# Paired PSUM banks, a sum of squares on VectorE and Newton steps for 1/sqrt in a hybrid decoder layer

## The chip, the core and the metric

The kernel runs on one core of one Trainium2 chip. The metric is device time in microseconds. PE is TensorE (matrix products), PEld its loading of weights, DVE is VectorE, ACT is ScalarE, POOL is GpSimd and SP is SyncE, which issues the DMAs. SBUF is the on-chip working memory, PSUM the eight accumulator banks that PE writes.

## The reference

One decoder layer over 1024 tokens of 1024 features, all in float32:

```
u = rmsnorm(x, g_mix);  z = u @ w_in            # split into x_rnn, x_gate, c_q, c_kv, k_rope
y_rnn = rglru(x_rnn) * gelu(x_gate)             # convolution, gates, linear recurrence
q, k, v from rmsnorm(c_q) @ w_q_up, rmsnorm(c_kv) @ w_kv_up, rotary parts
for each of 8 query blocks of 128 tokens, 8 heads:
    pr = softmax(causal(q @ k.T * scale));  y_att = pr @ v
h = x + concat(rmsnorm(y_rnn), rmsnorm(y_att)) @ w_out
h = h + (silu(rmsnorm(h) @ w_gate) * (rmsnorm(h) @ w_up)) @ w_down
h = h + sigmoid(rmsnorm(h) @ w_ple_gate) * rmsnorm(p @ w_ple_proj)
return rmsnorm(h, g_final)
```

Each `rmsnorm` is `y * rsqrt(mean(y*y) + 1e-6) * g`.

## The kernel before

**Tiling.** Activations lie transposed: features on the 128 partitions, 1024 tokens along the free axis, so a layer width of 1024 is 8 tiles of 128x1024. A float32 product is done as three fp32r products: both operands are split in a high and a low part (`x_h`, `x_l`, `w_h`, `w_l`), and hi·hi, hi·lo and lo·hi are added in PSUM (`mm`). The high part is a copy on ACT, the low part a subtraction on DVE. A PSUM bank holds 512 float32 columns, so 1024 tokens take two matmuls into two banks.

**Stages.** A loop over k = 0..7 loads a tile of x, splits it, and multiplies it with the first two column tiles of w_in (`g1`, shown as `g_a`, `g_b`). Beside it ACT squares the tile and POOL adds the squares up in `x_acc` (`sq_acc`). `x_acc` gives the norm of x (`nx`). Meanwhile PE takes the next tile of w_in (`in_mm(0)`, tile name `wn`). When the row of 1/sqrt values has been spread over the partitions (`nx_rb`), `evac` multiplies it onto the results in PSUM, which frees the banks. Then come the other w_in tiles and the recurrence (to about 175 us in the profile), attention (175 to 375), the output projection, FFN gate and up (475 to 850), FFN down (to about 1075), the gated per-layer embedding ("PLE", 1075 to 1228) and the last norm with the stores.

**A norm** (`rstd_part`): PE transposes the accumulated squares (`*_ms`), DVE reduces them (`n_ss`) and makes the mean (`n_m`), ACT takes the square root (`n_rt`), DVE takes the reciprocal and refines it by one Newton step in four small operations (`n_r`, `n_t`), PE transposes the result back, spread over partitions (`*_bc`), and ACT copies it to SBUF (`*_rb`). Eleven such chains run: `nx`; `nk` and `nq` (latents); `nr` and `na` (the two mixer halves); `nf` (FFN); `ne` and `np` (PLE); and `no` three times (chunks of the tokens at the end). The square root needs another activation table on ACT than Sin, Exp or Sigmoid do; changing it is an ACT_TABLE_LOAD.

**Attention.** `scores(hd, qb)` makes the scores of 128 queries against n = 128(qb+1) keys in chunks of at most 512 columns, one bank each. A block with n over 512 ("wide": 4 of the 8 blocks of a head, 32 in all) has two chunks. For each chunk DVE reduces the negative maximum into `nm`; for two chunks DVE takes the smaller of both in a one-column operation. ACT then does Exp for each chunk with an accumulated sum (each followed by an ACTIVATION_READ_ACCUMULATOR) into `pA`, `pA3` or `pB`. `tav_steps` transposes the weights on PE (`tp`), copies and splits them (`pf`, `pt`; part of the subtractions on POOL), and multiplies with v (`av`).

**What sets the order.** No instruction is written out directly: class `Plan` records each operation, prices it with a cost table (`cost`), and a list scheduler (`order`) lays out the program of each engine. The key of an operation is its place in the code plus small offsets (`OFF`); a tile waits for a free buffer of its tag, where tag "bank" has the 8 PSUM banks. All instructions are issued from one line (L361), so tile names tell them apart.

Of the kernel before, what the change touches and what calls it, by code (L numbers as in the profile page):

```python
# [141 lines left out]
class Plan:  # L142


    def __init__(self, nc):
        self.nc, self.ops, self.tags, self.hold = nc, [], {}, None
        self.engines = {n: getattr(nc, n) for n in ("vector", "scalar", "gpsimd", "tensor", "sync")}
# [20 lines left out]
    def cost(self, eng, fn, a, k, out):  # L168
# [34 lines left out]
    def add(self, eng, fn, a, k):  # L203
# [23 lines left out]
        o.key = o.idx + OFF.get(eng[0] + out.buf.name.rstrip('_ab') if isinstance(out, View) else '', 0) + (DEF if eng in ('vector', 'scalar') and not any(v.buf.tag == 'bank' for v in ins + outs) else 0)  # L227
# [11 lines left out]
    def order(self):  # L239
# [28 lines left out]
        while left:  # L268
            while frees and frees[0][0] <= t:
                _, _, tag, n = heapq.heappop(frees)  # L270
                free[tag] += n
            moved = False
            for e in names:
# [29 lines left out]
                o = best[2]  # L303
                moved = True
# [8 lines left out]
                for b in o.bufs:  # L313
# [3 lines left out]
                    free[b.tag] -= 1  # L317
# [9 lines left out]
                for b in o.bufs:  # L327
                    b.left -= 1
                    b.done = max(getattr(b, "done", 0.0), o.end)
                    if not b.left:  # L330
                        heapq.heappush(frees, (b.done, b.pos, b.tag, 1))
# [20 lines left out]
    def emit(self):  # L352
        for o in self.order():
            for b in o.bufs:
                if b.real is not None:
                    continue
                pool, shape, dt = b.args
                b.real = pool.tile(shape, dt, name=b.name, tag=b.tag, bufs=b.cap)
# [9 lines left out]
VA = ()  # L368
VS = ()
# [6 lines left out]
def hybrid_layer(ctx, tc, xT, pT, pos, vec, const, const2, w1, wn, wrg, wq, wkv, wo, wg, wu, *rest):  # L376
# [140 lines left out]
    def rstd_part(acc, n, name, res, copy=True):  # L517
# [4 lines left out]
        ss, m, rt, r0, t, r = (small([P, 8], "n_" + c)[:, :nb] for c in ("ss", "m", "rt", "r0", "t", "r"))  # L522
# [95 lines left out]
    g1 = [pair("g1") for _ in range(2)]  # L618
    acc = slot("x_acc")
    xs = []  # L620
    for k in range(8):
# [25 lines left out]
        sq_acc(acc, xr, k == 0, V if k in VA else G, k in VS)  # L647
# [10 lines left out]
    def in_mm(i, mid=None):  # L658
        wh, wl = weight(("wn", i), 2 if i < 9 else 0)
        pss = pair("wn")  # L660
# [5 lines left out]
        return pss  # L666

    def evac(pss, dst):
        for h in range(2):
            V.tensor_mul(dst[:, HS[h]], pss[h], rxs[0][:, HS[h]])  # L670
# [11 lines left out]
    evac(g1[0], ckv)  # L682
    krz = slot("krz")
    evac(g1[1], krz)
# [177 lines left out]
    def scores(hd, qb):  # L862
        if qb == 0:
            pA, pA3 = slot("pA"), slot("pA3")
            st[hd] = {"p": {0: pA[:, 0:128], 1: pA[:, 128:384], 2: pA[:, 384:768], 3: pA3[:, 0:512]},
                      "rs": small([P, 2, 8], "rs"), "nm": small([P, 8, 2], "nm")}
# [6 lines left out]
        chunks = [(c0, min(c0 + HB, n)) for c0 in range(0, n, HB)]  # L873
        pss = []
        for i, (c0, c1) in enumerate(chunks):
            w = c1 - c0
            ps = bank("s")
            pss.append(ps)
            T.matmul(ps[:, :w], lhsT=qh[:, cc], rhs=kh[:, c0:c1], start=True, stop=False)
            T.matmul(ps[:, :w], lhsT=qh[:, cc], rhs=kl[:, c0:c1], start=False, stop=False)  # L880
            if c1 == n:
                T.matmul(ps[:, w - P:w], lhsT=ib, rhs=mb, start=False, stop=False)
            T.matmul(ps[:, :w], lhsT=ql[:, cc], rhs=kh[:, c0:c1], start=False, stop=True)
# [3 lines left out]
        for i, (c0, c1) in enumerate(chunks):  # L887
            A.activation(pd[:, c0:c1], pss[i][:, :c1 - c0], AF.Exp, bias=nm[:, qb, 0:1], accum_out=rs[:, i, qb:qb + 1])

    def tav_steps(hd, hf):  # L890
# [29 lines left out]
        def fin():  # L920
# [418 lines left out]
    def gate_out(i, ps):  # L1339
# [152 lines left out]
```

## Time and profile before

| | us |
|---|---|
| three runs: fastest, median, slowest | 1241.95, 1243.89, 1246.2 |
| the profiled execution's own time | 1246.8 |
| its span | 1245.0 |
| PE busy in the span | 1178.9 (95%) |
| DVE busy | 1016.7 (82%) |
| ACT busy | 653.1 (52%) |
| POOL busy | 335.2 (27%) |

Busy time of PE is that of overlapping matmuls, so a stretch in which PE is shown as busy can still hold small gaps. The stage matters more than the mean: PE is nearly without idle time in most stages, and stands idle at the start, in attention, at the change from gate/up to down, and at the very end.

### The profile page before, as it was taken

Reading aid. Unit: us, or ns where it says so; the run is one execution under the profiler, and the core shown is the slowest. Engines: PE = TensorE matmul, PEld = TensorE weight load, DVE = VectorE, ACT = ScalarE, POOL = GpSimd, SP = SyncE. Lnnn points to the kernel's source line nnn. Section 1 sums busy time; section 2 is a strip of 40 time slices with the busy share of each in tenths; the row PEclk is TensorE's granted clock in tenths of the full one; section 3 lists DMA queues with packets and bytes.
Section 4 is the critical chain, followed back from the end, with each engine's and each line's share of the span. In section 5 each row is a group of like instructions: output and inputs, shape, how many; then the busy total and the mean of one; then the engine's idle time right before and its main releaser. Section 6 shows DMA issues by size and latency. Waiting matters only on the chain.

```text
span 1245.0 us, 15659 instructions
## 1 busy us (share of the span) xinstructions
PE 1178.9 (95%) x5608; PEld 972.0 (78%) x5608; DVE 1016.7 (82%) x1564; ACT 653.1 (52%) x1154; POOL 335.2 (27%) x204
## 2 busy tenths in 40 slices
PE   5999999988989999999999999999699999999995
PEld 4788886866768878888888888888478787888894
DVE  7878797887896989988988888867678676985998
ACT  8338767866774655544444444435222222566565
POOL 6002133564550423331233321233000000244042
PEclk8899999999999999999999999999799999999998
DMA  8100100000031531434344343465997666032352
GB/s 299 47 2 33 51 1 1 2 1 1 34 118 34 204 132 38 167 142 164 119 153 186 128 160 143 162 212 184 378 412 263 239 238 245 27 106 81 117 189 102
DMA packets 50271, 165.36 MB, mean 133 GB/s; under 512 B 5649, under 2 KB 8977, under 8 KB 50193
## 3 DMA queue, kind: packets, MB, share of 16 engines
q1 hardware_dynamic: 50192, 164.37, 36.0%
q8 instruction: 44, 0.72, 0.2%
q14 instruction: 35, 0.28, 0.1%
HBM read 115.58 MB, written 48.76 MB: 132 GB/s over the span
## 4 chain that ended last, share of the span: by engine, by line
PE 71%; DVE 11%; issue 7%; ACT 6%; DMA 3%; POOL 2%; SPq 0%; DVEq 0%; POOLq 0%; ACTq 0%
PE ff_z L361 27%; PE ff_y L361 13%; PE ff_x L361 6%; PE s L361 3%; PE wo_a L361 3%; PE wo_b L361 3%; PE wn_b L361 3%; PE wn_a L361 2%; PE av L361 2%; PE tp L361 2%; DMA wd_r<-in_wd 1%; PE qps L361 1%; DVE nm L361 1%; POOL h L361 1%; DVE pt L361 1%
## 5 line engine op out<-in xcount | busy, mean ns | idle before, releaser
L361 POOL TENSOR_TENSOR silu<-silu,nf_rb 128x512 f32<-128x512 f32 x77 | 120.0, 1584 | 279.6 <-DVE silu L361 258.0
L361 PE MATMUL ff_z<-hx,wd 128*128 128x512 f32 x528 | 129.6, 393 | 11.2 <-DVE h L361 8.7
L361 PE MATMUL ff_z<-x,wg 128*128 128x512 f32 x528 | 128.2, 390 | 0.5 <-DVE x L361 0.5
L361 PE MATMUL ff_z<-x,wu 128*128 128x512 f32 x528 | 127.0, 389 | 0.0
L361 PEld LDWEIGHTS ff_z<-hx,wd 128*128 128x128 f32 x528 | 99.6, 190 | 34.6 <-DVE h L361 9.9
L361 PEld LDWEIGHTS ff_z<-x,wg 128*128 128x128 f32 x528 | 98.9, 188 | 21.5 <-DVE x L361 0.9
L361 PEld LDWEIGHTS ff_z<-x,wu 128*128 128x128 f32 x528 | 99.1, 188 | 20.6
L361 POOL TENSOR_TENSOR p_acc<-p_acc,sq 128x1024 f32<-128x1024 f32 x7 | 19.8, 2825 | 232.9 <-ACT sq L361 232.6
L361 POOL TENSOR_TENSOR pt<-pf,pt 128x512 fp32r<-128x512 f32 (+1 forms) x48 | 58.9, 1233 | 66.5 <-DVE pt L361 27.7
L361 ACT ACTIVATE wd<-wd_r 128x384 fp32r<-128x384 f32 (+1 forms) x64 | 29.9, 492 | 76.5 <-DMA wd_r<-in_wd 30.2
L361 DVE TENSOR_TENSOR h<-ff_z,h 128x512 f32<-128x512 f32 x64 | 43.9, 687 | 29.8 <-PE ff_z L361 21.4
L361 PE MATMUL ff_y<-hx,wd 128*128 128x512 f32 x264 | 66.5, 395 | 0.1
L361 PE MATMUL ff_y<-x,wg 128*128 128x512 f32 x264 | 64.1, 390 | 0.6 <-ACT x L361 0.6
L361 PE MATMUL ff_y<-x,wu 128*128 128x512 f32 x264 | 63.4, 389 | 0.0
L361 PE MATMUL plg<-hg_h,wpg_l 128*128 128x256 f32 (+1 forms) x192 | 61.1, 319 | 1.3 <-DVE wpg_l L361 1.2
L361 PE MATMUL plg<-hg_h,wpg_h 128*128 128x256 f32 (+1 forms) x192 | 61.5, 320 | 0.0
L361 PE MATMUL plg<-hg_l,wpg_h 128*128 128x256 f32 (+1 forms) x192 | 61.2, 319 | 0.0
L361 ACT ACTIVATE wd<-wd_s 128x384 fp32r<-128x384 f32 (+1 forms) x48 | 23.8, 497 | 69.4 <-DVE wd_s L361 47.9
L361 PEld LDWEIGHTS ff_y<-hx,wd 128*128 128x128 f32 x264 | 50.3, 191 | 11.2 <-issue 0.7
L361 PEld LDWEIGHTS ff_y<-x,wg 128*128 128x128 f32 x264 | 49.5, 188 | 11.4 <-ACT x L361 1.0
L361 PEld LDWEIGHTS ff_y<-x,wu 128*128 128x128 f32 x264 | 49.6, 188 | 10.3
L361 PE MATMUL av<-pt,v 128*128 128x512 f32 (+1 forms) x192 | 51.5, 367 | 5.1 <-DVE pt L361 3.3
(391 smaller groups left out, 3219.4 us busy)
## 6 DMA issues: line engine op xcount, KB each, us to landing
hx<-hx SPq DMA_DIRECT2D x154, 512.0 KB, 3.7
wpg_raw<-in_wpg SPq DMA_DIRECT2D x24, 512.0 KB, 3.5
wg_r<-in_wg SPq DMA_DIRECT2D x22, 512.0 KB, 4.9
wu_r<-in_wu SPq DMA_DIRECT2D x22, 512.0 KB, 4.1
wd_r<-in_wd SPq DMA_DIRECT2D x24, 384.0 KB, 6.8
wn_raw<-in_wn SPq DMA_DIRECT2D x10, 512.0 KB, 3.5
wo_raw<-in_wo SPq DMA_DIRECT2D x8, 512.0 KB, 3.7
h<-in_xT SPq DMA_DIRECT2D x8, 512.0 KB, 4.2
```

The costliest lines, as they stand in the source:

```text
L361: getattr(self.engines[o.eng], o.fn)(*a, **k)
```

## The change

1. **PSUM in pairs.** The eight banks are allocated as four tiles of 128x1024 (`banks*`). A new tile `wide()` takes both banks of one pair, and a single-bank tile is placed in a half-used pair first (`seat`). `g1`, `in_mm` and wide score blocks use `wide()`. `evac` is then one multiplication over 1024 columns, and a wide score block has one maximum and one Exp over all its columns, with no one-column minimum and no second sum.
2. **Sums of squares of x** are added by DVE, not POOL. Their keys are put 40 later (`XLATE`).
3. **1/sqrt** is made on DVE alone: a seed from the bits of the number, then three Newton steps of three operations. A chain has 10 small DVE operations where it had 5, and there are no square roots on ACT.
4. **The planner** no longer starts an operation on an engine other than PE if a small one (cost under 0.25) with a key lower by more than 20 will be ready within 0.3 (`HOLD`). The price of an accumulated sum on ACT is raised.

Counts: PE has the same matmuls and SP the same 345 instructions; DVE goes from 1564 to 1542, ACT (without table loads) from 1033 to 989, POOL from 200 to 193.

```diff
     def tile(...)            # Tile.__init__
+        self.units, self.at = (2 if tag == "bank" and shape[1] > 512 else 1), None
...
-            c += 0.093 * sum(isinstance(k.get(n), View) for n in ("scale", "bias", "accum_out"))
+            c += 0.093 * sum(isinstance(k.get(n), View) for n in ("scale", "bias"))
+            c += 0.2 * isinstance(k.get("accum_out"), View)
...
-        o.key = o.idx + OFF.get(...)
+        o.key = o.idx + self.shift + OFF.get(...)
...
+        def seat(b):
+            if b.units == 2:
+                return next((i for i in range(0, len(banks), 2) if banks[i] and banks[i + 1]), None)
+            alone = [i for i, f in enumerate(banks) if f and not banks[i ^ 1]]
+            return alone[0] if alone else next((i for i, f in enumerate(banks) if f), None)
...
-                    ok = all(b.placed or free[b.tag] > min(unplaced(b), RES.get(b.tag, 99)) for b in o.bufs)
+                    ok = all(b.placed or free[b.tag] - b.units >= min(unplaced(b), RES.get(b.tag, 99))
+                             and (b.tag != "bank" or seat(b) is not None) for b in o.bufs)
...
+                soon = next((r for r, _, x in future[e][:6] if r < t + HOLD and r + 0.05 < t + o.cost
+                             and x.cost < 0.25 and x.key + 20 < best[0]), None) if e != "tensor" else None
+                if soon is not None:
+                    heapq.heappush(avail[e], (best[1], o.idx, o))
+                    continue
...
+                if b.tag == "bank":
+                    if b.at // 2 not in self.pairs:
+                        n = f"banks{b.at // 2}"
+                        self.pairs[b.at // 2] = pool.tile([P, 2 * HB], F32, name=n, tag=n, bufs=1)
+                    c = b.at % 2 * HB
+                    b.real = self.pairs[b.at // 2][:, c:c + b.units * HB]
+                    continue
...
+XLATE = 40
+HOLD = 0.3
...
+    def wide(name):
+        return plan.tile(psp, [P, S], F32, name, "bank", 8)
...
-        A.activation(rt, m, AF.Sqrt)
-        V.reciprocal(r0, rt)
-        V.tensor_mul(t, r0, r0)
-        V.tensor_mul(t, t, m)
-        V.tensor_scalar(t, t, -0.5, 1.5, op0=ALU.mult, op1=ALU.add)
-        V.tensor_mul(r, r0, t)
+        V.tensor_scalar(r0.bitcast(I32), m.bitcast(I32), -0.5, 1597463007.0, op0=ALU.mult, op1=ALU.add)
+        for _ in range(3):
+            V.tensor_mul(t, r0, r0)
+            V.scalar_tensor_tensor(out=t, in0=t, scalar=-0.5, in1=m, op0=ALU.mult, op1=ALU.mult)
+            V.scalar_tensor_tensor(out=r0, in0=t, scalar=1.5, in1=r0, op0=ALU.add, op1=ALU.mult)
...
-        sq_acc(acc, xr, k == 0, V if k in VA else G, k in VS)
+        plan.shift = XLATE
+        sq_acc(acc, xr, k == 0, V)
+        plan.shift = 0
...
-        for h in range(2):
-            V.tensor_mul(dst[:, HS[h]], pss[h], rxs[0][:, HS[h]])
+        V.tensor_mul(dst, ps, rxs[0])
...
-            V.tensor_reduce(out=nm[:, qb, i:i + 1], in_=ps[:, :w], axis=AX.X, op=ALU.max, negate=True)
-        if len(chunks) == 2:
-            V.tensor_tensor(out=nm[:, qb, 0:1], in0=nm[:, qb, 0:1], in1=nm[:, qb, 1:2], op=ALU.min)
-        for i, (c0, c1) in enumerate(chunks):
-            A.activation(pd[:, c0:c1], pss[i][:, :c1 - c0], AF.Exp, bias=nm[:, qb, 0:1], accum_out=rs[:, i, qb:qb + 1])
+        V.tensor_reduce(out=nm[:, qb:qb + 1], in_=ps[:, :n], axis=AX.X, op=ALU.max, negate=True)
+        A.activation(pd[:, :n], ps[:, :n], AF.Exp, bias=nm[:, qb:qb + 1], accum_out=rs[:, qb:qb + 1])
```

**DVE in the loop over the tiles of x.** Names: `x_l` and `w_l` are the low parts, `x_acc` the sum of squares. Before:

```order
L361 SCALAR_TENSOR_TENSOR x_l<-xr,vc,x_h 128x1024
L361 TENSOR_TENSOR w_l<-w_raw,w_h 128x256 x4
L361 SCALAR_TENSOR_TENSOR x_l<-xr,vc,x_h 128x1024
L361 TENSOR_TENSOR w_l<-w_raw,w_h 128x256
L361 SCALAR_TENSOR_TENSOR x_l<-xr,vc,x_h 128x1024
L361 TENSOR_TENSOR w_l<-w_raw,w_h 128x256
L361 SCALAR_TENSOR_TENSOR x_l<-xr,vc,x_h 128x1024
```

With the change:

```order
L390 SCALAR_TENSOR_TENSOR x_l<-xr,vc,x_h 128x1024
L390 TENSOR_TENSOR w_l<-w_raw,w_h 128x256 x3
L390 TENSOR_TENSOR x_acc<-x_acc,sq 128x1024
L390 TENSOR_TENSOR w_l<-w_raw,w_h 128x256
L390 SCALAR_TENSOR_TENSOR x_l<-xr,vc,x_h 128x1024
L390 TENSOR_TENSOR w_l<-w_raw,w_h 128x256
L390 TENSOR_TENSOR x_acc<-x_acc,sq 128x1024
L390 SCALAR_TENSOR_TENSOR x_l<-xr,vc,x_h 128x1024
L390 TENSOR_TENSOR w_l<-w_raw,w_h 128x256
L390 SCALAR_TENSOR_TENSOR x_l<-xr,vc,x_h 128x1024
```

Two of the seven additions stand between the splits here, the other five stand further behind; the last two have one operation of the rotary tables between them, and after one more comes the reduction of the norm.

**PE in attention, at the first transposes of a head's wide blocks.** Before, the first row is the last scores matmul of a narrow block, and the last row reads a wide block's weights (`pB`):

```order
L361 MATMUL s<-k_h,q_l 128x512
L361 MATMUL tp<-cs,pA 128x128 x2
L361 MATMUL tp<-cs,pA_1504 128x128
L361 MATMUL tp<-cs,pA 128x128
L361 MATMUL tp<-cs,pA_1504 128x128
L361 MATMUL qps<-cq_h,wq_h 128x512
L361 MATMUL qps<-cq_l,wq_h 128x512
L361 MATMUL qps<-cq_h,wq_l 128x512
L361 MATMUL qps<-cq_h,wq_h 128x512
L361 MATMUL qps<-cq_l,wq_h 128x512
L361 MATMUL qps<-cq_h,wq_l 128x512
L361 MATMUL tp<-cs,pA_1504 128x128
```

With the change (the row ahead of the first is the last scores matmul of a wide block, 1024 columns in `banks_90`; the last row reads three wide blocks' weights):

```order
L390 MATMUL banks_297<-cs,pA_1401 128x128
L390 MATMUL banks_391<-k_h,q_h 128x128
L390 MATMUL banks_391<-k_l,q_h 128x128
L390 LDWEIGHTS ib
L390 MATMUL banks_391<-mb,ib 128x128
L390 MATMUL banks_391<-k_h,q_l 128x128
L390 MATMUL banks_297<-k_h,q_h 128x256
L390 MATMUL banks_297<-k_l,q_h 128x256
L390 LDWEIGHTS ib
L390 MATMUL banks_297<-mb,ib 128x128
L390 MATMUL banks_297<-k_h,q_l 128x256
L390 MATMUL banks_391<-cs,pB 128x128 x3
```

Two query projections' matmuls no longer stand between scores and transposes here; the next head's narrow scores do.

**DVE near the end, in the norm of the second chunk.** Names: `n_r`, `n_t`, `n_m` are the norm's small tiles, `gt`, `e`, `o_acc` belong to the PLE gate. Before:

```order
L361 RECIPROCAL n_r_10647<-n_rt 128x2
L361 TENSOR_TENSOR o_acc<-o_acc,o_sq 128x256
L361 TENSOR_TENSOR n_t<-n_r_10647 128x2
L361 TENSOR_TENSOR gt<-plg,np_rb 128x256
L361 TENSOR_TENSOR n_t<-n_t,n_m 128x2
L361 TENSOR_TENSOR o_acc<-o_acc,o_sq 128x256
L361 TENSOR_SCALAR n_t<-n_t 128x2
L361 TENSOR_TENSOR gt<-plg,np_rb 128x256
L361 TENSOR_TENSOR n_r<-n_r_10647,n_t 128x2
```

With the change:

```order
L390 TENSOR_SCALAR n_r_9984<-n_m 128x2
L390 TENSOR_TENSOR n_t<-n_r_9984 128x2
L390 SCALAR_TENSOR_TENSOR n_t<-n_t,n_m 128x2
L390 SCALAR_TENSOR_TENSOR n_r_9984<-n_t,n_r_9984 128x2
L390 TENSOR_TENSOR n_t<-n_r_9984 128x2
L390 TENSOR_TENSOR o_acc<-o_acc,o_sq 128x256
L390 SCALAR_TENSOR_TENSOR n_t<-n_t,n_m 128x2
L390 SCALAR_TENSOR_TENSOR n_r_9984<-n_t,n_r_9984 128x2
L390 TENSOR_TENSOR n_t<-n_r_9984 128x2
L390 SCALAR_TENSOR_TENSOR n_t<-n_t,n_m 128x2
L390 SCALAR_TENSOR_TENSOR n_r_9984<-n_t,n_r_9984 128x2
```

The small operations stood one by one between larger ones; now ten stand nearly in a row.

## Rows read from the trace of the kernel before

**Rows 1.** Busy time by stage: us, PE, PEld, DVE, ACT, POOL (instructions), PE clock, DMA, GB/s.
```profile
0.00:41.00 41.00, 27.17 (x86) 21.14 (x87) 33.55 (x25) 28.27 (x34) 19.76 (x12) 0.83 0.68 249
69.00:175.00 106.00, 105.89 (x482) 87.53 (x482) 89.28 (x104) 67.59 (x79) 16.43 (x6) 1.00 0.07 25
175.00:375.00 200.00, 182.33 (x1046) 145.86 (x1045) 165.31 (x328) 144.44 (x359) 99.43 (x72) 0.99 0.07 25
...
1228.00:1245.00 17.00, 1.87 (x9) 0.90 (x7) 11.49 (x27) 4.89 (x11) 5.56 (x7) 0.64 0.35 123
```

**Rows 2.** Waits of PE over the span: us in total, times, longest.
```profile
PE g_a L361 <- DVE x_l L361: 8.3, 2, 5.2
PE no_ms L361 <- DVE o_acc L361: 7.6, 2, 7.2
...
PE tp L361 <- ACT pB L361: 3.4, 5, 1.4
```

**Rows 3.** Timeline of DVE, then of POOL, in the x loop: start, us, operation.
```profile
10.67 5.82 DVE L361 TENSOR_TENSOR w_l<-w_raw,w_h 128x256 fp32r<-128x256 f32 x4
...
28.11 4.07 DVE L361 SCALAR_TENSOR_TENSOR x_l<-xr,vc,x_h 128x1024 fp32r<-128x1024 f32 x1
32.09 0.41 DVE L361 TENSOR_TENSOR w_l<-w_raw,w_h 128x256 fp32r<-128x256 f32 x1
32.43 1.27 DVE L361 SCALAR_TENSOR_TENSOR x_l<-xr,vc,x_h 128x1024 fp32r<-128x1024 f32 x1
...
11.14 16.76 POOL L361 TENSOR_TENSOR x_acc<-x_acc,sq 128x1024 f32<-128x1024 f32 x6 [10.70 <-ACT sq L361]
```

**Rows 4.** Busy time in a stretch behind an idle PE (columns as in rows 1).
```profile
32.20:38.00 5.80, 5.77 (x14) 4.57 (x15) 5.80 (x8) 3.29 (x3) 0.00 (x0) 0.50 0.29 90
```

**Rows 5.** Timeline of DVE, ACT and PE around the norm of x.
```profile
54.35 0.17 DVE L361 TENSOR_SCALAR n_m<-n_ss 128x8 f32<-128x8 f32 x1
...
60.47 1.28 ACT L361 ACT_TABLE_LOAD   x1
61.76 0.20 ACT L361 ACTIVATE q<-q 128x4 f32<-128x4 f32 x1
...
63.19 0.60 ACT L361 ACTIVATE nx_rb<-nx_bc 128x512 f32<-128x512 f32 x1 [0.74 <-PE nx_bc L361]
...
68.60 0.39 PE L361 MATMUL wn_b<-x_h,wn_l 128*128 128x512 f32 x1
68.82 0.39 PE L361 MATMUL wn_a<-x_h,wn_h 128*128 128x512 f32 x1
```

**Rows 6.** Timeline of DVE and PE in the last norm.
```profile
1236.90 0.17 DVE L361 TENSOR_SCALAR n_m<-n_ss 128x2 f32<-128x2 f32 x1
...
1237.54 0.16 DVE L361 TENSOR_TENSOR n_t<-n_r 128x2 f32<-128x2 f32 x1
1237.74 0.16 DVE L361 TENSOR_TENSOR n_t<-n_t,n_m 128x2 f32<-128x2 f32 x1
...
1238.35 0.69 PE L361 MATMUL no_bc<-cs,n_r 128*128 128x128 f32 x2 [1.94 <-DVE n_r L361]
```

**Rows 7.** Groups by form, 175 to 390 us: busy us, mean ns | idle before.
```profile
L361 POOL TENSOR_TENSOR pt<-pf,pt 128x512 fp32r<-128x512 f32 x32 | 44.0, 1380 | 34.1 <-DVE pt L361 14.0 <-PE tp L361 11.3 <-DVE nm L361 7.9
L361 DVE TENSOR_REDUCE nm<-s 128x1 f32<-128x512 f32 x48 | 32.4, 680 | 1.6 <-PE s L361 1.5
...
L361 ACT ACTIVATE pB<-s,nm 128x512 f32<-128x512 f32 x40 | 27.4, 686 | 21.0 <-DVE nm L361 20.9
...
L361 DVE TENSOR_TENSOR nm<-nm 128x1 f32<-128x1 f32 x32 | 12.0, 374 | 0.3
...
L361 DVE TENSOR_REDUCE nm<-s 128x1 f32<-128x128 f32 x16 | 4.4, 278 | 1.7 <-PE s L361 1.5
```

**Rows 8.** The tile nm, its one-column minimum: ns min/median/max, first and last start.
```profile
L361 DVE TENSOR_TENSOR nm<-nm x32: 141/153/2294, 190.4 to 357.7; 128x1 f32<-128x1 f32 x32
```

**Rows 9.** Busy time from the PLE gate's last part to DVE's last sum (columns as in rows 1).
```profile
1146.46:1235.60 89.14, 80.40 (x542) 74.10 (x540) 86.90 (x150) 60.95 (x103) 19.99 (x16) 0.98 0.37 131
```

More of the change, by code (lines that the diff above doesn't have):

```diff
@@ L226, in add @@
             v.buf.log = keep
-        o.key = o.idx + OFF.get(eng[0] + out.buf.name.rstrip('_ab') if isinstance(out, View) else '', 0) + (DEF if eng in ('vector', 'scalar') and not any(v.buf.tag == 'bank' for v in ins + outs) else 0)
+        o.key = o.idx + self.shift + OFF.get(eng[0] + out.buf.name.rstrip('_ab') if isinstance(out, View) else '', 0) + (DEF if eng in ('vector', 'scalar') and not any(v.buf.tag == 'bank' for v in ins + outs) else 0)
         o.bufs = list(dict.fromkeys(v.buf for v in ins + outs))
@@ L256, in order @@
         frees = []
+        banks = [True] * free.get("bank", 0)
+        def seat(b):
[3 more added lines that the diff above has]
+            return alone[0] if alone else next((i for i, f in enumerate(banks) if f), None)
         for o in self.ops:
@@ L269, in order @@
             while frees and frees[0][0] <= t:
-                _, _, tag, n = heapq.heappop(frees)
-                free[tag] += n
+                _, _, tag, b = heapq.heappop(frees)
+                free[tag] += b.units
+                if tag == "bank":
+                    banks[b.at:b.at + b.units] = [True] * b.units
             moved = False
@@ L316, in order @@
                     b.placed = True
-                    free[b.tag] -= 1
+                    free[b.tag] -= b.units
+                    if b.tag == "bank":
+                        b.at = seat(b)
+                        banks[b.at:b.at + b.units] = [False] * b.units
                     q, d = queue[b.tag], ahead[b.tag]
@@ L330, in order @@
                     if not b.left:
-                        heapq.heappush(frees, (b.done, b.pos, b.tag, 1))
+                        heapq.heappush(frees, (b.done, b.pos, b.tag, b))
                 for s in o.succ:
@@ L521, in rstd_part @@
         nb = w // P
-        ss, m, rt, r0, t, r = (small([P, 8], "n_" + c)[:, :nb] for c in ("ss", "m", "rt", "r0", "t", "r"))
+        ss, m, r0, t = (small([P, 8], "n_" + c)[:, :nb] for c in ("ss", "m", "r0", "t"))
         for b0 in range(0, nb, 4):
@@ L615, in tables @@
         tabs.extend((sc, cse, cpos, cneg))
-    g1 = [pair("g1") for _ in range(2)]
+    g1w = [wide("g1") for _ in range(2)]
+    g1 = [[w[:, HS[0]], w[:, HS[1]]] for w in g1w]
     acc = slot("x_acc")
@@ L659, in in_mm @@
         wh, wl = weight(("wn", i), 2 if i < 9 else 0)
-        pss = pair("wn")
+        ps = wide("wn")
+        pss = [ps[:, HS[0]], ps[:, HS[1]]]
         for k in range(8):
@@ L665, in in_mm, with evac @@
                 mid()
-        return pss
-    def evac(pss, dst):
-        for h in range(2):
-            V.tensor_mul(dst[:, HS[h]], pss[h], rxs[0][:, HS[h]])
+        return ps
+    def evac(ps, dst):
+        V.tensor_mul(dst, ps, rxs[0])
     cq0p = in_mm(0, lambda: next(nx))
@@ L681, in hybrid_layer @@
     ckv = slot("ckv")
-    evac(g1[0], ckv)
+    evac(g1w[0], ckv)
     krz = slot("krz")
-    evac(g1[1], krz)
+    evac(g1w[1], krz)
     cq = [slot("cq0"), slot("cq1")]
@@ L872, in scores @@
         cc = slice(qb * P, (qb + 1) * P)
-        chunks = [(c0, min(c0 + HB, n)) for c0 in range(0, n, HB)]
-        pss = []
-        for i, (c0, c1) in enumerate(chunks):
[L876 to L880, printed above, removed]
-            if c1 == n:
-                T.matmul(ps[:, w - P:w], lhsT=ib, rhs=mb, start=False, stop=False)
-            T.matmul(ps[:, :w], lhsT=ql[:, cc], rhs=kh[:, c0:c1], start=False, stop=True)
-            V.tensor_reduce(out=nm[:, qb, i:i + 1], in_=ps[:, :w], axis=AX.X, op=ALU.max, negate=True)
-        if len(chunks) == 2:
-            V.tensor_tensor(out=nm[:, qb, 0:1], in0=nm[:, qb, 0:1], in1=nm[:, qb, 1:2], op=ALU.min)
-        for i, (c0, c1) in enumerate(chunks):
-            A.activation(pd[:, c0:c1], pss[i][:, :c1 - c0], AF.Exp, bias=nm[:, qb, 0:1], accum_out=rs[:, i, qb:qb + 1])
+        ps = wide("s") if n > HB else bank("s")
+        for c0 in range(0, n, HB):
+            c1 = min(c0 + HB, n)
+            T.matmul(ps[:, c0:c1], lhsT=qh[:, cc], rhs=kh[:, c0:c1], start=True, stop=False)
+            T.matmul(ps[:, c0:c1], lhsT=qh[:, cc], rhs=kl[:, c0:c1], start=False, stop=False)
+            if c1 == n:
+                T.matmul(ps[:, n - P:n], lhsT=ib, rhs=mb, start=False, stop=False)
+            T.matmul(ps[:, c0:c1], lhsT=ql[:, cc], rhs=kh[:, c0:c1], start=False, stop=True)
+        V.tensor_reduce(out=nm[:, qb:qb + 1], in_=ps[:, :n], axis=AX.X, op=ALU.max, negate=True)
+        A.activation(pd[:, :n], ps[:, :n], AF.Exp, bias=nm[:, qb:qb + 1], accum_out=rs[:, qb:qb + 1])
     def tav_steps(hd, hf):
```

20 lines of the change are left out of this document (7 added, 13 removed).

## Prediction

> **What bounds the kernel now.** First the busy time by stage. From 69 to 175 us PE is busy 105.89 of 106 us: nothing on another engine can shorten that stretch, and a later start of it is a later end. PE has room in three places: the start (27.17 of 41 us busy), attention (182.33 of 200) and the end (1.87 of 17) [rows 1]. Then PE's waits, which say for whom: at the start for `x_l` of DVE (8.3 us in two waits), at the end for the last sum `o_acc` (7.6), in attention for many short ones, of which `tp` for ACT's `pB` (3.4 in 5) is one that the change touches [rows 2]. Then the timelines of those places.
>
> At the start DVE is the late engine, and it is late because POOL adds `x_acc` at the same time. From 10.67 to 32.1 us it does only six `w_l` and three `x_l`. A split of 128x1024 takes 4.07 us there and 1.27 us as soon as POOL is silent; four `w_l` take 5.82 us beside POOL and one takes 0.41 alone; POOL's additions take 16.76 us for six [rows 3]. Undisturbed, the nine operations would be 6 x 0.41 + 3 x 1.27 = 6.3 us, so some 15 us are lost.
>
> **Part 1, the start.** Of `x_acc`, POOL's seven additions go and DVE gets seven. I price one at 1.27 us, the two-operand DVE operation of the same size that runs alone [rows 3]. From 10.67 us to its last addition DVE then has, by the changed order, 7 `w_l` (2.9), 6 `x_l` (7.6), 7 additions (8.9) and twelve operations of 1024 columns for tables and for the next weights (1.27 at most each, fewer where there is one operand; I take 1.0, so 12): 31 us, less about 2 for the overlap of successive operations (32.43 starts 0.07 before 32.09 + 0.41 ends). That ends at 40 us. With PE's transposes and two reductions more it is near 42.3, where `n_m` is now at 54.35 [rows 5]. The 1/sqrt chain is then ten dependent DVE operations, 0.20 us apart as in the chain at the end (1237.54, 1237.74) [rows 6], with `n_m` 2.2 us: 44.5. The spread row `nx_rb` is ready near 46 and not at 63.8, without the table load of 60.47 on the way [rows 5]. PE has done `g1` and `wn` 0 by then, waits some 3 to 4.5 us for banks, and begins `wn` 1 at 46.1. This takes 48 matmuls at 0.227 (68.60, 68.82): 10.9 us, to 57.0. Now it ends at 68.8 [rows 5]. The gain is 11.8 at most. Against it: behind an idle PE the granted clock is 0.50, the lower of the two levels, and 14 matmuls take 5.77 us [rows 4], 0.41 each. If this follows the new wait, up to 3.4 us are lost, so the gain is 8.4 to 11.8. I take **-10**; since the stretch from 69 us is full, it stays. Bounds -3 (rival (c)) and -13.
>
> **Part 2, attention.** Each of 32 wide blocks loses one reduction's fixed cost, one minimum and one Exp with its sum. The reduction's slope is (680 - 278)/384 = 1.05 ns a column, so a fixed cost of 278 - 134 = 144 ns; the minimum has a mean of 374 ns [rows 7], with a median of 153 and one at 2294 [rows 8]. That is 32 x (0.144 + 0.15 to 0.374): 9 to 17 us of DVE time, and the same count of ACT's operations. PE idles 17.7 us there [rows 1], so 18 is the most that can come off. How much does, hangs on the waits: DVE is busy 165 of 200 us, ACT 144, and neither ends every wait. I take a third to a half of the DVE saving, about -6.
>
> Against it works the order. A wide block's first transpose needs reduction and Exp of the whole block now: near 1.2 us (1.05 x 1024 + 144 ns) and 1.1 us (between one and two of 0.686 [rows 7]), one behind the other, where the first chunk could go ahead before. Meanwhile the PE work that the program places between a block's last scores matmul and its first transpose shrinks. Priced with 0.227 us for 512 columns, and in proportion for fewer, it falls from 10.0 to 7.3 us in the mean of the 32 blocks and from 4.0 to 2.6 at the least; 12 blocks are under 5, none before under 4. The first three wide blocks of head 0 in the excerpt have 2.6 to 3.9. With 2.3 us of pure work plus handoffs and queues on DVE and ACT, some of these will make PE wait. This is within the -6, and its ends are -18 and +15 (0.65 more of a wait in each wide block).
>
> **Part 3, the norms.** Five more small DVE operations a chain, eleven chains. `nk`, `nq`, `nr`, `na` and `nf` stand beside PE work that is full or counted above: 0, with +1 at most for `nf`, where DVE is dense. At the end DVE is the bound: it is busy 86.90 of 89.14 us up to its last sum [rows 9]. There the chains of the chunks cost now little more than 0.1 us an operation between larger ones; ten in a row, each waiting for the one before, take 2.0. That is +1.2 for each of two chunks, +1 for `ne` and `np` together. The last chain from `n_m` (1236.90) to `no_bc` (1238.35) takes 1.45 us [rows 6], and will take 11 x 0.20 = 2.2: +0.75. Back come DVE's short waits on ACT around the table loads of 1.28 us, of which 2.24 us of idle [rows 9] is all there is: -1.6. Sum **+2.5**, ends 0 and +5. A load is followed at once by the next ACTIVATE (60.47 + 1.28 = 61.75; 61.76) [rows 5], so its price is 1.28.
>
> The Trainium skill ("ScalarE: Activation LUTs", section "What ACT_TABLE_LOAD costs") counts about 2.66 us for each switch, the load and a drain of 1.38 behind it. By the page two loads at the end would be 5.3 us and the sum there could come near 0; the trace shows no drain, so the sum goes by the row.
>
> **Part 4, the rest.** `evac` with one operation for two saves 12 starts, beside a full PE: 0. `HOLD` moves work by tenths; what it moves is in the orders above. FFN and PLE have the same PE and DMA order: 0.
>
> **The sum** against the profiled execution: 1246.8 - 10 - 6 + 2.5 = 1233.3. That execution is 2.9 above the median of the three runs, so on the median 1243.9 - 13.5 = **1230**. The forecast's own range, from the start's 8.4 to 11.8, attention's 0 to -12 and the end's 0 to +5, is 1224 to 1237.
>
> **Rivals.** A measurement of this kernel can tell about 0.3%, 3.7 us, from no change: faster is under 1240.2, slower over 1247.6.
>
> (a) *Attention gives all of it.* If each DVE operation there was on the path, -18 for -6: 1218. For it speaks ACT's 20.9 us of waiting for `nm` [rows 7]; against it that PE's own wait for `pB` is 3.4 [rows 2].
>
> (b) *The shorter cover decides.* Place: the first transpose of each wide block. Price: 32 x p, where p is the extra wait of PE in a block. The rest of the sum is -13.5, so at p = 0.42 nothing is left (1230 + 13.4 = 1243, same) and from p = 0.54 the kernel is slower; with p = 0.65 it is 1251. For it: reduction and Exp of 2.3 us against a cover of 2.6 to 5 in 12 blocks. Against: 20 blocks have 6 us and more, so those 12 would have to wait over 1.4 us each to reach the end on the other side.
>
> (c) *The start's gain is not there.* If with POOL silent ACT's copies or the DMA of x pace the loop, or PE idles at half clock longer, the gain is 3: 1237. Against: by the rows DVE alone lost 15 us.
>
> (d) *Newton beside POOL.* The small `nm` operation that took 2294 ns against a median of 153 [rows 8] shows that a small two-operand DVE operation can be held; POOL's `pt` operations beside it take 1380 ns [rows 7]. The nine two-operand steps of `nr` and `na` run there. Nine held for 1.38 would be 12.4; half of that on the path is +6: 1236. The Trainium skill ("SBUF — State Buffer", section "Who interferes with whom") has the rule: a DVE operation with two SBUF inputs contends with a GpSimd one that reads SBUF, and the lock holds for a whole instruction. The trace agrees, in the 4.07 against 1.27 us of `x_l` [rows 3] too.
>
> **How the numbers follow.** Forecast 0.50 (1230), (a) 0.17 (1218), (c) 0.09 (1237), (d) 0.07 (1236), (b) at the same time 0.10 (1243), (b) slower 0.07 (1251). Faster 0.83, same 0.10, slower 0.07. The range runs from 1214, (a) with the start's best end, to 1242, half way into (b); outside are the slow end of (b) and small tails.
>
> **What would show it.** In the changed profile `x_l` is near 1.3 us throughout, `n_m` of the first norm is near 42 us, and `wn` 2 starts at 57 to 60; if it is later than 64, part 1 is wrong. From 69 us on the same work is 10 us earlier up to 175. In attention the reductions over 1024 take near 1.2 us, and PE's waits for `pB` and `pt` tell (a) from (b): under 8 us together for (a), over 20 for (b). At the end PE's last wait for `n_r` grows from 1.94 us to some 2.7, and DVE's window of 89.14 us grows by 1 to 3. A total over 1242 with an early start would make the order in attention the error; one with a late start, the pace of the x loop.

## The result and the profile after

The changed kernel takes 1561.7 us (median of four, 1560.3 to 1564.1) against 1244.8 for the kernel before: a ratio of 1.255, 95% interval 1.252 to 1.258. The prediction was 1230 within 1214 to 1242, with 0.07 for slower. The forecast was a gain; the change is a loss, larger than in any of the prediction's cases.

The page of the changed kernel, its busy times (us, share of the span, instructions):

```profile
PE 1277.1 (82%) x5608; PEld 954.1 (61%) x5608; DVE 982.7 (63%) x1542; ACT 631.5 (40%) x1067; POOL 300.4 (19%) x197
```

DVE and ACT have less work than before, as intended, and PE has the same 5608 matmuls. What grew is above all time in which PE is idle: 66 us of the span before (1245.0 - 1178.9), 285 now (1562.3 - 1277.1). Its busy time grew too, by 98 us for the same matmuls; the single wait below shows why. By stage (columns as in [rows 1]), first before, then after:

```profile
475.00:850.00 375.00, 375.00 (x1660) 310.71 (x1659) 315.73 (x429) 174.83 (x302) 109.44 (x70) 1.00 0.41 152
```

```profile
69.00:175.00 106.00, 98.66 (x424) 78.45 (x423) 79.55 (x91) 64.63 (x74) 14.84 (x6) 0.95 0.08 25
175.00:375.00 200.00, 161.55 (x869) 119.80 (x867) 118.81 (x214) 110.82 (x241) 74.87 (x59) 0.99 0.00 1
475.00:850.00 375.00, 311.61 (x1266) 228.97 (x1265) 244.20 (x340) 136.48 (x235) 83.75 (x53) 1.00 0.28 105
```

In FFN gate and up, where before PE was busy for 375.00 of 375 us, it now gets 1266 matmuls into the time of 1660. The 106 us that were full before ([rows 1]) are not full either. The loss is spread over the whole program, and most of it lies in stages that the prediction had put at 0 (a table by stage stands with the experiments). PE's waits (us in total, times, longest) of the changed kernel, the answer to [rows 2]:

```profile
PE banks L390 <- DVE h L390: 75.6, 91, 7.9
PE banks L390 <- DVE silu L390: 40.5, 51, 0.9
PE banks L390 <- DVE ff_u L390: 23.7, 30, 0.9
PE banks L390 <- ACT silu L390: 23.0, 33, 1.4
PE banks L390 <- ACT ff_u L390: 21.3, 31, 0.7
```

All of PE's waits together were 59.2 us in 41 places; they are 278.4 us in 365. The new ones are short, alike, and behind the operations that take a result out of PSUM. One of them in the timeline, DVE first, then PE (start, us, operation, idle time and what ended it):

```profile
604.61 0.69 DVE L390 TENSOR_TENSOR silu<-banks,silu 128x512 f32<-128x512 f32 x1 [1.68 <-PE banks L390]
```

```profile
604.18 0.39 PE L390 MATMUL banks<-x,wg 128*128 128x512 f32 x1
605.36 3.72 PE L390 MATMUL banks<-x,wg 128*128 128x512 f32 x15 [0.78 <-DVE silu L390]
```

PE has ended one group of matmuls and begun the next, in the other half of the same pair, with the matmul at 604.18. DVE reads the ended group's result from 604.61 to 605.30, and PE's next matmul, at 605.36, starts only when that is done, though it doesn't write the bank that DVE reads. Start to start it is 1.18 us where matmuls follow each other at 0.23 (1660 in 375.00 us above), so this stop costs 0.95 us, more than the 0.78 of idle time, because the matmul before it takes 0.39 us by itself and no successor overlaps with it.

What PE waits for there can be read from the built program: a wait names a semaphore (a counter that one engine raises and another waits on) and a value, and the value names the instruction. Of PE's waits for DVE or ACT in the changed kernel, 423 name an instruction that shares with the matmul nothing but the tile: it reads the other bank of the pair. In the kernel before no two banks share a tile, and there is no such wait. In the other direction, 401 waits of DVE or ACT for PE name a matmul into a bank that they don't read. The layer that turns tiles into semaphores took each pair tile as one thing.

### The profile page after: what moved, and what is told of

Read it like the earlier page. It is cut to its first block, busy times and chain, and to the rows that moved or that the text cites. A ratio compares the mean times of both kernels' runs of the same rounds, so it can differ in the third digit from the quotient of the medians.

```text
span 1562.3 us, 15519 instructions
## 1 busy us (share of the span) xinstructions
PE 1277.1 (82%) x5608; PEld 954.1 (61%) x5608; DVE 982.7 (63%) x1542; ACT 631.5 (40%) x1067; POOL 300.4 (19%) x197
## 4 chain that ended last, share of the span: by engine, by line
PE 70%; DVE 17%; ACT 8%; issue 3%; DMA 1%; SPq 0%; DVEq 0%; ACTq 0%
PE banks L390 70%; DVE h L390 5%; DVE silu L390 2%; DVE ff_u L390 1%; ACT silu L390 1%; ACT ff_u L390 1%; DVE nm L390 1%; ACT pf L390 1%; DVE pt L390 1%; DVE gt L390 1%; ACT e L390 1%; DVE xc L390 1%; DVE k_l L390 1%; DVE wpg_l L390 1%; DVE n_ss L390 0%
## 5 line engine op out<-in xcount | busy, mean ns | idle before, releaser
L390 PE MATMUL banks<-hx,wd 128*128 128x512 f32 x924 | 239.9, 406 | 76.2 <-DVE h L390 72.0
L390 PE MATMUL banks<-x,wg 128*128 128x512 f32 x924 | 234.7, 401 | 55.1 <-DVE silu L390 31.8
L390 PE MATMUL banks<-x,wu 128*128 128x512 f32 x924 | 234.1, 400 | 52.5 <-DVE ff_u L390 23.7
L390 PEld LDWEIGHTS banks<-hx,wd 128*128 128x128 f32 x924 | 168.2, 190 | 147.5 <-DVE h L390 107.1
L390 PEld LDWEIGHTS banks<-x,wg 128*128 128x128 f32 x924 | 167.6, 188 | 119.8 <-DVE silu L390 48.8
L390 PEld LDWEIGHTS banks<-x,wu 128*128 128x128 f32 x924 | 167.9, 188 | 116.1 <-DVE ff_u L390 36.7
L390 DVE TENSOR_TENSOR h<-banks,h 128x512 f32<-128x512 f32 x128 | 87.4, 690 | 149.8 <-PE banks L390 141.8
L390 PE MATMUL banks<-hg_h,wpg_l 128*128 128x256 f32 (+1 forms) x192 | 62.9, 330 | 5.4 <-DVE wpg_l L390 2.8
L390 PE MATMUL banks<-hg_h,wpg_h 128*128 128x256 f32 (+1 forms) x192 | 63.5, 331 | 4.2 <-DVE gt L390 3.4
L390 PE MATMUL banks<-hg_l,wpg_h 128*128 128x256 f32 (+1 forms) x192 | 63.0, 328 | 4.0 <-DVE gt L390 3.5
L390 PE MATMUL banks<-pt,v 128*128 128x512 f32 (+1 forms) x192 | 56.0, 376 | 11.3 <-DVE k_l L390 2.8
```

What stands on the lines that cost most here:

```text
L390: getattr(self.engines[o.eng], o.fn)(*a, **k)
```

## The experiments

**The theories.** T: the waits are placed for a whole pair tile, so matmuls into one half and the reading of the other half alternate. R1: single banks are placed into half-used pairs first (`seat`), so that a bank comes back too soon. R2: one of the three other parts (Newton steps, sums of squares on DVE, `HOLD`) does it. The counts of 431, 467 and 142 in the expectations take in some waits for other columns of the same bank; for another bank alone they are 423, 458 and 133.

**e1, one tile for all eight banks.** The same instructions, order and banks as the change:

```diff
-                    if b.at // 2 not in self.pairs:
-                        n = f"banks{b.at // 2}"
-                        self.pairs[b.at // 2] = pool.tile([P, 2 * HB], F32, name=n, tag=n, bufs=1)
-                    c = b.at % 2 * HB
-                    b.real = self.pairs[b.at // 2][:, c:c + b.units * HB]
+                    if 0 not in self.pairs:
+                        self.pairs[0] = pool.tile([P, 8 * HB], F32, name="banks", tag="banks", bufs=1)
+                    c = b.at * HB
+                    b.real = self.pairs[0][:, c:c + b.units * HB]
```

> The changed kernel with the same instructions in the same order on the same eight banks, but the banks are slices of one tile of 128x4096 and not of four tiles of 128x1024. In its program PE waits for readers of its own bank alone. Theory T (a wait is placed for the whole pair tile: a matmul into one half waits for the reader of the other half, and the reader waits for matmuls of the other half): PE's 365 waits of 278 us fall to about 60 us, and the time to 1230, the sum of the prediction, within 1215 to 1245. Rival R1 (banks are reused too soon, because single tiles are placed into half-used pairs first): the placement is the same, so 1560. Rival R2 (the three other parts: Newton steps, sums of squares on DVE, HOLD): 1560.

Measured: 1224.8 us (1223.7 to 1226.5), ratio to before 0.984 (0.982 to 0.985). FFN gate and up is full again, and none of PE's largest waits is of the new kind:

```profile
455.00:830.00 375.00, 374.99 (x1654) 310.06 (x1653) 319.26 (x431) 173.57 (x302) 106.76 (x69) 1.00 0.42 152
```

```profile
PE banks L389 <- DVE h L389: 8.8, 3, 7.7
PE banks L389 <- ACT x_h L389: 5.6, 1, 5.6
PE banks L389 <- DVE n_r L389: 4.6, 2, 2.7
```

R1 and R2 fall: the placement, the Newton steps, the sums and `HOLD` are all still there. T stands, with a surprise inside: with one tile of eight banks PE's waits are placed by bank (none for another bank alone), with pair tiles by tile.

**e2, pairs alone.** The kernel before, its banks made halves of pairs; every operation as narrow as it was and in its old place. Which bank a result gets follows the change's `seat` (that part of the edit is left out here):

```diff
+                if b.tag == "bank":
+                    if b.at // 2 not in self.pairs:
+                        n = f"banks{b.at // 2}"
+                        self.pairs[b.at // 2] = pool.tile([P, 2 * HB], F32, name=n, tag=n, bufs=1)
+                    c = b.at % 2 * HB
+                    b.real = self.pairs[b.at // 2][:, c:c + HB]
+                    continue
```

> The kernel before with nothing changed but that its eight banks are halves of four pair tiles, placed by the rule of the change; all operations stay narrow and in their order. PE has 467 waits for readers of the other half alone (431 in the changed kernel). Theory T: the time of the change or a little more, 467 x 0.76 us above 1244 at most, so 1500 to 1600. Rival R1: slower too. Rival R2: 1244.

Measured: 1617.1 us, ratio 1.299 (1.293 to 1.304). So pair tiles with the change's placement cost 372 us in the kernel before, without any other part of the change; that it is the tiles and not the placement, e1 shows. The same wait leads its list:

```profile
PE banks L378 <- DVE h L378: 76.1, 91, 8.0
PE banks L378 <- DVE silu L378: 42.2, 53, 0.9
```

**e3, two tiles of four banks** in the changed kernel (`g` is 4):

```diff
-                        self.pairs[b.at // 2] = pool.tile([P, 2 * HB], F32, name=n, tag=n, bufs=1)
-                    c = b.at % 2 * HB
-                    b.real = self.pairs[b.at // 2][:, c:c + b.units * HB]
+                        self.pairs[b.at // g] = pool.tile([P, g * HB], F32, name=n, tag=n, bufs=1)
+                    c = b.at % g * HB
+                    b.real = self.pairs[b.at // g][:, c:c + b.units * HB]
```

> The changed kernel with two tiles of 128x2048 (four banks each) in place of four pairs; order and banks as in the change. PE has 605 waits for readers of other banks alone, 174 more than in the change. Theory T: slower than the change by 174 x 0.76 = 132 us, about 1690. Rivals R1 and R2: 1560, as nothing that they name changes.

Measured: 1862.0 us, ratio 1.495 (1.488 to 1.503): the direction that T alone expects, and more than its 1690. PE waits 421.3 us in 531 places. Beside that, its clock falls, which the estimate left out. The page's clock row (tenths of full speed, 40 slices):

```profile
PEclk9999666856566799999999999999888999999998
```

In attention, where PE now stops most often, the mean granted clock of a slice lies between the two levels of 1.2 and 2.4 GHz, and over the span it is 0.895 against 0.982 for the change.

**e12, an empty pair first.** The changed kernel with its four pairs and `seat` turned round. As `seat` also decides when a wide tile finds room, the planner's order differs in places from that of the change:

```diff
-            alone = [i for i, f in enumerate(banks) if f and not banks[i ^ 1]]
-            return alone[0] if alone else next((i for i, f in enumerate(banks) if f), None)
+            whole = [i for i, f in enumerate(banks) if f and banks[i ^ 1]]
+            return whole[0] if whole else next((i for i, f in enumerate(banks) if f), None)
```

> The changed kernel, four pair tiles kept, but a single bank is placed in an empty pair first and in a half-used one last (the change does the opposite). PE has 142 waits for readers of the other half alone, not 431. Theory T: in the change 339 more waits of PE than in e1 cost 337 us, so 0.99 each, and 339 of 431 placed waits made PE stop; at that rate 142 x 339/431 x 0.99 = 111 us above e1, 1336; less if the neighbour's reader is already done when the wait comes, down to e1's 1225. If wide blocks now find no empty pair, attention shows it: over e1's 160 us from the first scores matmul to the output projection.

Measured: 1273.4 us, ratio 1.023 (1.021 to 1.025). Most of the loss is gone with most of the waits, but 48.6 us above e1 stay; the estimate of 111 was an upper end. PE stops 52 times more than in e1, which at 0.95 us each is 49. Attention takes 195 us from the first scores matmul to the first of the output projection, against 160 in e1: that is where most of it lies. Together:

| kernel | PE's placed waits for another bank alone | PE's waits in the profile | median us |
|---|---|---|---|
| e1, one tile | 0 | 45.8 us in 26 | 1224.8 |
| e12, pairs spread | 133 | 75.2 us in 78 | 1273.4 |
| after, pairs | 423 | 278.4 us in 365 | 1561.7 |
| e2, before in pairs | 458 | 307.2 us in 392 | 1617.1 |
| e3, fours | 605 | 421.3 us in 531 | 1862.0 |

From e1 to the change PE stops 339 times more and the span grows by 339.6 us (1222.7 to 1562.3). The stop read above is a typical one and not the mean: idle time grew by 232.6 us, 0.69 a stop. As PE's order is the same in both, the two traces can be compared matmul by matmul. From start to start, the 357 places where PE stands idle in the change alone cost 302.4 us (0.85 each), and the matmul that follows each of them comes 0.10 us late, which is another 35.1. That is 337.5 us, all but some 2 of the difference. In e2 and e3 the span grows by more for each further stop, 1.06 us (against the kernel before) and 1.25 (against e1); their granted clock is lower, 0.970 and 0.895, and how much of it the clock took was not worked out.

The Trainium skill ("PSUM — Partial Sum Buffer", section "PSUM bank collisions raise a hardware error") says that two engines must not be in the same bank and the same quadrant of partitions at once, and that accesses to different banks run cleanly side by side. The runs agree: e1 lets PE write the bank next to the one that DVE reads, and takes 336.9 us less. The chip did not ask for these waits.

**e4, the three other parts without pairs.** Banks are tiles of their own, scores and `evac` in chunks of 512 as before:

```diff
+        plan.shift = XLATE
+        sq_acc(acc, xr, k == 0, V)
+        plan.shift = 0
...
+HOLD = 0.3
...
+        V.tensor_scalar(r0.bitcast(I32), m.bitcast(I32), -0.5, 1597463007.0, op0=ALU.mult, op1=ALU.add)
```

> The kernel before with the three other parts of the change (sums of squares on DVE, Newton steps, HOLD) and no pairs: each bank a tile of its own, scores and evac in chunks of 512. Theory T with the prediction's own terms: 1244 - 10 + 2.5 = 1236, between 1231 and 1243. Rival R1: 1236 too. Rival R2: near 1560.

Measured: 1240.0 us, ratio 0.996 (0.994 to 0.997). R2 falls again.

**The terms one by one.** e5 has the wide operations alone (banks as in e1), e6 the sums of squares on DVE alone, e7 the Newton steps alone, all against the kernel before; e8 is e1 with ACT's square root (the planner's higher price of an accumulated sum is in all four). For e5, from the kernel before:

```diff
-        pss = pair("wn")
+        ps = wide("wn")
...
+        V.tensor_reduce(out=nm[:, qb:qb + 1], in_=ps[:, :n], axis=AX.X, op=ALU.max, negate=True)
+        A.activation(pd[:, :n], ps[:, :n], AF.Exp, bias=nm[:, qb:qb + 1], accum_out=rs[:, qb:qb + 1])
```

> The kernel before with the wide operations alone (banks as slices of one tile as in e1; sums of squares on POOL, square root on ACT, no HOLD). In e1 the stretch from the first to the last scores matmul is 151.7 us where before has 168.6. If the wide blocks alone do that, attention gives 13 to 17 and the time is 1229 to 1233; the prediction's term of -6 gives 1239. If wide operations also cost at the start (evac waits for both halves), up to 3 more.

For e6, from the kernel before:

```diff
-        sq_acc(acc, xr, k == 0, V if k in VA else G, k in VS)
+        plan.shift = XLATE
+        sq_acc(acc, xr, k == 0, V)
+        plan.shift = 0
```

> The kernel before with the sums of squares of x on DVE alone (keys 40 later, no pairs, square root on ACT, no HOLD). The prediction's part 1 without Newton steps: n_m near 42 us and not 54.35, then the chain by ACT and DVE of before, 5.7 us and not 2.2: the start gives 6 to 8, time 1237. If the Newton steps are what brings the start forward, it gives under 3 and 1243.

For e7, from the kernel before:

```diff
-        A.activation(rt, m, AF.Sqrt)
-        V.reciprocal(r0, rt)
...
+        V.tensor_scalar(r0.bitcast(I32), m.bitcast(I32), -0.5, 1597463007.0, op0=ALU.mult, op1=ALU.add)
+        for _ in range(3):
```

> The kernel before with the Newton steps alone (no pairs, sums of squares on POOL, no HOLD). By the prediction: +2.5 at the end; the start gains up to 3 as the chain behind n_m is shorter and no table load of 1.28 stands in it: 1243 to 1248. If small DVE operations are held behind POOL in attention (rival d), +6 more: 1250.

For e8, from e1:

```diff
-        V.tensor_scalar(r0.bitcast(I32), m.bitcast(I32), -0.5, 1597463007.0, op0=ALU.mult, op1=ALU.add)
-        for _ in range(3):
...
+        A.activation(rt, m, AF.Sqrt)
+        V.reciprocal(r0, rt)
```

> e1 (one tile, wide operations, sums of squares on DVE, HOLD) with the square root on ACT again. If the Newton steps pay at the start (about 3) and cost at the end (1 to 3), it stays within 2 of e1's 1224.8; if they cost on the whole, it is faster, 1222; if the start needs them, 1230.

Measured: e5 1243.7 (ratio 0.998, 0.997 to 1.000), e6 1236.9 (0.992, 0.990 to 0.995), e7 1250.7 (1.004, 1.002 to 1.005), e8 1226.0 (0.984, 0.981 to 0.986). So R2's parts by themselves cost little: e6 comes out as expected, e8 within 2 of e1, and e7 above its range, at the 1250 that stands there for rival (d). e5 misses: attention and output projection gain 11.8, but what stands ahead of them loses 10.1. Where each kernel gains and loses, from PE's timeline in the profiled executions (us; a stage runs from its first matmul to the next one's):

| | start to scores | scores to FFN | FFN and down to PLE | PLE to end |
|---|---|---|---|---|
| before | 181.4 | 274.8 | 675.4 | 113.4 |
| after, pairs | 188.3 | 318.8 | 923.0 | 132.2 |
| e1, all, one tile | 174.7 | 258.9 | 674.5 | 114.6 |
| e4, no pairs | 167.3 | 279.5 | 674.2 | 114.9 |
| e5, wide alone | 191.5 | 263.0 | 674.2 | 113.5 |
| e6, sums on DVE alone | 169.2 | 276.6 | 676.3 | 113.5 |
| e7, Newton alone | 179.0 | 278.7 | 673.8 | 113.0 |
| e8, e1 without Newton | 176.5 | 258.7 | 674.3 | 114.1 |
| e9, e1 with w_in narrow | 170.1 | 258.5 | 673.8 | 114.6 |
| e10, scores wide alone | 181.7 | 260.2 | 673.9 | 113.8 |
| e11, e1 with HOLD 0 | 180.9 | 258.8 | 674.2 | 113.1 |

**e9, e10 and e11.** e9 and e10 ask whether it is the wide results of w_in that cost at the start, e11 what `HOLD` is worth. Of e1, e9 changes this alone (and the first two results, `g1`, in the same way); e10 has it too, with sums, square root and `HOLD` as before:

```diff
-        ps = wide("wn")
+        pss = pair("wn")
...
-        V.tensor_mul(dst, ps, rxs[0])
+        for h in range(2):
+            V.tensor_mul(dst[:, HS[h]], pss[h], rxs[0][:, HS[h]])
```

> e1 (one tile of eight banks, all parts) but with w_in's products and evac in single banks as before; only score blocks over 512 are wide. Theory W (a wide result of w_in holds two banks until one long evac is done, and PE waits for that): the projections go as in e4, scores start at 167 us and not 175, attention takes e1's 160, the time is 1217. Rival: single banks break up the pairs and scores wait for them: 1224 or more.

> The kernel before with wide score blocks alone (one tile of eight banks, w_in narrow, sums of squares on POOL, square root on ACT, no HOLD): the term of attention by itself. With e5's 162.6 us from the first scores matmul to the output projection in place of 180.0: 1244 - 17 = 1228. With the prediction's -6: 1239.

For e11, from e1:

```diff
-HOLD = 0.3
+HOLD = 0.0
```

> e1 with HOLD at 0, so without the rule that keeps engines free. If the rule does what it is written for, small steps start later and the time is 3 to 8 above e1's 1224.8; if it moves work by tenths, as the prediction says, 1223 to 1227.

Measured: e9 1220.6 us, ratio 0.981 (0.979 to 0.983), the fastest kernel of this study; e10 1236.8 (0.994, 0.992 to 0.996); e11 1228.5 (0.987, 0.986 to 0.989). e9 has its scores at 170.1 us, 4.6 earlier than e1; 167 was expected. The stretch behind the norm of x, e1 and then e9:

```profile
41.00:69.00 28.00, 25.88 (x113) 20.84 (x112) 19.64 (x57) 9.43 (x11) 3.35 (x1) 0.94 0.06 19
69.00:175.00 106.00, 102.53 (x465) 83.63 (x463) 88.78 (x105) 70.11 (x84) 18.81 (x8) 1.00 0.08 25
```

```profile
41.00:69.00 28.00, 28.00 (x137) 23.22 (x136) 26.00 (x67) 12.18 (x13) 3.34 (x1) 1.00 0.06 19
69.00:170.00 101.00, 98.45 (x439) 80.46 (x438) 86.92 (x108) 67.85 (x81) 19.07 (x8) 1.00 0.08 27
```

In e1 PE idles from 42 to 44 us, and the granted clock falls with it (0.94); in e9 PE is full there. The start of the next result of w_in, first in e1, then in e9:

```profile
45.32 1.28 PE L389 MATMUL banks<-x_h,wn_h 128*128 128x512 f32 x2 [0.22 <-ACT nx_rb L389]
```

```profile
42.61 0.39 PE L389 MATMUL banks<-x_h,wn_h 128*128 128x512 f32 x1
```

Three results hold six banks by then. In e1 the next wide result needs the last two at once, and the norm's own transposes are in them, so it starts behind ACT's copy `nx_rb`; in e9 it starts 2.7 us earlier, in one bank, while the norm goes through the other. So a wide result costs time here because it holds and needs two banks; what PE waits for is the norm, and not a long `evac`, as theory W had it. From 69 us on both have gaps where before had none ([rows 1]), and why is open. e10 shows attention's term alone: 14.6 us by the table. The profiled executions of e10 and e7, by which the table was made, are the fastest of their runs (1231.6 of 1231.6 to 1238.9, and 1246.5 of 1246.5 to 1255.9). By the medians e10 gains 7.6 us and e7 loses 5.5, so for these two the table shows less of a cost than the times do. e11 loses 6 us before the scores: `HOLD` is worth 3.7 us in e1, though the prediction gave it tenths.

## Why the prediction was wrong

**The step that failed** is in part 4: "FFN and PLE have the same PE and DMA order: 0". The order was the same and the conclusion was not, because what an instruction waits for is no part of its place in the row. The change of the allocation was followed only in what it does to the plan (which banks are free, what can be wide, how far a transpose stands behind its scores), and never in what the tile means to the layer that places semaphores. That a pair tile could be tracked as one thing was no rival, and so no range held it. It is worth 1561.7 - 1224.8 = 336.9 us, 25 times the whole predicted gain. By stage, from e1 to the change, 248.5 us of it are in FFN and down and 17.6 from PLE on, which part 4 put at 0; 59.9 are in attention and the output projection and 13.6 before, so parts 1 and 2 lack the same term.

Nothing in the trace of before shows it, for no PSUM tile there holds two results. The program of the changed kernel does: the number of waits is nearly the same as before, but not what they name.

**The rest of the sum** can be held against e1, which is the change without that cost: 1224.8, just inside the forecast's own range of 1224 to 1237. That is partly luck, as the start gave less and attention more than was forecast; and the range has a flaw of its own, for its three ends added up give 1220 to 1240.5.

*Part 1, the start: -10 predicted.* DVE's part of the working holds row by row. Answering [rows 3] and [rows 5], e1 has DVE's last addition, the mean, and the spread row at:

```profile
38.09 1.23 DVE L389 TENSOR_TENSOR x_acc<-x_acc,sq 128x1024 f32<-128x1024 f32 x1
...
41.75 0.17 DVE L389 TENSOR_SCALAR n_m<-n_ss 128x8 f32<-128x8 f32 x1
...
44.67 1.09 ACT L389 ACTIVATE nx_rb<-banks 128x512 f32<-128x512 f32 x2 [0.22 <-PE banks L389]
```

The forecast was 40, 42.3 and near 46; it is 39.3, 41.75 and 45.8. `wn` 2 begins at 57.75 (57 to 60 forecast, 68.82 before). The first matmul of wkv is 9.3 us earlier. The clock's loss was put at up to 3.4 us, while its row ([rows 4]) gives 2.6 (5.77 for 14 matmuls of 0.227); in e1 six matmuls from 45.32 to 48.11 us lose 1.4. "Since the stretch from 69 us is full, it stays" fails in e1, where the gain has shrunk to 6.7 us at the scores, and holds with narrow results of w_in (e9), where it is 11.3. So part 4's wide `evac`, "beside a full PE: 0", is a term mis-sized too: 4.6 us by e9. Rival (c) falls. e6 against e7 says which part brought it: the sums on DVE 12.2 us, the Newton steps 2.4.

*Part 2, attention: -6 predicted.* The mechanism was right and the size too small. With the output projection e1 gains 15.9 us (274.8 to 258.9), near the whole saving, as rival (a) had it. The bound of 18 for attention alone does not hold: from the first scores matmul to the output projection e1 takes 159.9 us instead of 180.0, and the output projection behind it gives 4.2 back. PE's busy time for the 957 matmuls there fell from 162.65 to 154.16, so part of what is shown as busy could come off too, which the bound left out. The new operations cost what was worked out from [rows 7] (1.2 and 1.1 us for 1024 columns):

```profile
L389 DVE TENSOR_REDUCE nm<-banks 128x1 f32<-128x1024 f32 x8 | 9.8, 1222 | 2.9 <-PE banks L389 2.7 <-ACT pB L389 0.2
L389 ACT ACTIVATE pB<-banks,nm 128x1024 f32<-128x1024 f32 x8 | 8.9, 1114 | 0.8 <-DVE nm L389 0.8
```

The shorter cover, the reason for taking a third, doesn't show in e1: PE's waits for `pB` are 1.0 us in one place, where they were 3.4 in 5 [rows 2]. Rival (b) falls. PE waits for `pt`, of DVE and POOL, for 5.3 us instead; with `pB` that is 6.3, under the 8 that was to speak for (a).

*Part 3, the norms: +2.5 at the end predicted.* It is +1.2 (113.4 to 114.6). The last chain takes the 2.2 us that were forecast against 1.45 in [rows 6], from `n_m` to the matmul:

```profile
1213.89 0.17 DVE L389 TENSOR_SCALAR n_m<-n_ss 128x2 f32<-128x2 f32 x1
...
1216.08 0.69 PE L389 MATMUL banks<-cs,n_r 128*128 128x128 f32 x2 [2.69 <-DVE n_r L389]
```

Rival (d), small steps held behind POOL, has its mechanism, and in e1 hardly a price. Steps of e1 in ns (min/median/max):

```profile
L389 DVE SCALAR_TENSOR_TENSOR n_r<-n_t,n_r x33: 160/166/1282, 42.6 to 1215.9; 128x8 f32<-128x8 f32 x24, 128x2 f32<-128x2 f32 x6, 128x4 f32<-128x4 f32 x3
```

The longest is 1282, the median 166. With narrow scores the Newton steps go with 3.9 us more between scores and FFN (e7, 278.7 against 274.8), with wide ones with 0.2 (e1 against e8). The granted clock of e7 in attention was 0.96 (179.0 to 363.3 us) and that of before 0.99 in [rows 1], which may be the cause; it was not tried. By its median e7 is 5.5 us slower than the kernel before (1250.7 against 1245.2), near rival (d)'s +6. Yet in its trace one of 33 such steps is long too (1108 ns), which pays for a fifth of that at most, so with narrow scores a cost of the Newton steps is measured and its cause is open.

*The sum.* In e1 the stages give -6.7 - 15.9 - 0.9 + 1.2 = -22.3 us of span, where -13.5 was forecast.

## What to carry to other kernels

When buffers are merged into one tile, ask first what the layer that places the waits tracks, the tile or its parts, and look in the built program at what each wait names: equal order and equal counts of waits say nothing about it. A new kind of short, even wait of the busiest engine behind every reader of its results was the mark of such a merged tile here, and a kernel in which only the tiles differ (e1) settles it at once. And price a change in every stage that uses the resource it touches, not in the stages it is meant for.

## What was not expected

One tile of eight banks is tracked bank by bank (e1: no wait of PE for another bank alone), tiles of two or four banks are tracked whole (423 and 605 such waits). Why the size decides is left open.

A stop of PE costs more than its idle time: 0.95 us from start to start where 0.78 is shown as idle, and 0.95 in the mean over all new stops once the late matmul behind each is counted (337.5 us for 357). And in e3, where stops are densest, the granted clock falls: 0.895 over its span, 0.982 in the change.
